# A decoder layer on one Trainium2 core: gate products on another engine, alternating buffers for weight sums, and another rule for when a unit is issued

## The chip, the cores and the metric

The kernel runs on one core of one Trainium2 chip. The metric is the device time of one execution in microseconds (us); three executions of the kernel before took 321.8, 321.82 and 323.23 us, with a median of 321.82 us. The engines of a core are called by the names of the profile: PE (matrix products), PEld (its weight loads, which overlap with PE), DVE (VectorE), ACT (ScalarE), POOL (GpSimd) and SP (here only an issuer of transfers).

## The reference

One decoder layer for 256 tokens of width 1024, all in float32:

```python
h = rms_norm(x)
q, k, v, ga | u, vb, gb | qc, gc | three merge gates = split(h @ w_in)
A = moba_attention(rope(q), rope(k), v) * silu(ga)        # 6 heads of 128
B = gmlp_spatial_gate(u, vb, w_spatial) * silu(gb)        # 6 groups of 128
C = memory_cross_attention(qc, rms_norm(mem) @ w_mem_kv) * silu(gc)   # 4 heads
m = sigmoid(ma) * (A @ w_a) + sigmoid(mb) * (B @ w_b) + sigmoid(mc) * (C @ w_c)
out = rms_norm(x + m @ w_out)
```

The products with `silu(...)` are the gate products of this document (branch B has one more, by the spatially mixed `vb`), and `ma`, `mb`, `mc` are the merge gates.

## The kernel before, in words

**Chunks.** The weights come as pieces of 128 x 2048 values, and each piece is used as two chunks of 128 x 1024, 124 chunks in all. PE's work is a fixed list of these chunks (`plan`): 0 to 3 are the memory's values, 4 to 7 its keys, 8 to 19 the values of A and the `vb` of B by token, 20 to 23 `qc`; then the features q, k, ub, gc, ga and gb two chunks at a time, with pairs of merge-gate chunks ("st") between them; from 88 on the branch projections ("br") with the last merge-gate pairs, and at the end the output projection.

**Splitting.** For precision every product of float32 is done in three passes of a faster type (fp32r): high by high, high by low, low by high. So each chunk is first split: ACT writes its high part (`hi`, L238, a copy into fp32r), then DVE its low part (`lo`, L242, the raw chunk minus `hi`). `hi` and `lo` have four buffers each, raw pieces three, and the program issues a chunk's split three chunks ahead of its products (LEAD). A few small products (transposes L724, scores of the first tokens L773, their values L821, spatial mixing L948) are plain fp32. The products of a chunk are L398 to L400 (by token, and the branch and output projections), L482 (merge gates) and L554 (features).

**Merge gates.** Each of the three gates (g = 0, 1, 2) is computed by a scheme with seven products in place of eight (i = 1, 2, 5, 3, 6, 7, 4 in the order of issue), each a pair of chunks. Products accumulate in two banks; when product 7 of a gate is done, DVE subtracts what the bank then holds from an earlier result (L498, the step called `c22`), and only then may product 4 go on adding in that bank. The sums of weight blocks that the products need are formed by transfers in two buffers, `form0` and `form1`: a block is loaded by SP's queue (L218) or added onto what the buffer holds by GpSimd's queue (L221). Which buffer a product uses is fixed by the product:

```python
    FORMS = {1: (0, 0), 5: (0, 1), 6: (0, 3), 4: (0, 2), 2: (1, 2), 7: (1, 1), 3: (1, 3)}
    BUF = {i: f[0] for i, f in FORMS.items()}
```

So product 4 of a gate and product 1 of the next, which are issued one after the other, both use `form0`, and the second is loaded only when both splits of the first have read it.

**The order of everything else.** All other work is cut into units (an engine, a cost in us, what it comes after, a chunk at which it is due). A planner, `Units`, keeps a clock for each engine while the program is written out: at each chunk it first lets in units of ACT, DVE, POOL and the queues, then the split of the chunk three ahead, then the chunk's products, then units of PE. A unit with its predecessors done is let in when the chunk has reached its due number, or when its engine's clock is at most 2.5 us (POOL 0.5 us) past PE's. Instructions run in the order in which they were written, engine by engine, so that a unit that waits holds back each split behind it.

**The gate products.** Each is over two heads or groups, 128 x 512 values: L959 for C (two of them) and A (three), L604 for B with its silu, L998 for B with the mixing. All eleven run on GpSimd. Their results are split for the branch projections by L964 on ACT (`ah`, `obh`, `och`) and L968 on DVE (`al`, `obl`, `ocl`). The sigmoids of the merge gates are L501 on ACT, and the first of them brings a load of the sigmoid table with it (`ACT_TABLE_LOAD`), because the silus before used another. On the way there also stand L350 and L351 on DVE (`dg`, four small instructions for the memory's norm), L403 (`mvl`, the low part of the memory's values) and L446 on GpSimd (sums of tokens for the merge gates).

The row names are those of the profile: `lo<-form,hi` is the low split of a merge-gate chunk, `lo<-raw,hi` that of any other.

Of the kernel before, what the change touches and what calls it, by code (L numbers as in the profile page):

```python
# [44 lines left out]

ORDER = (1, 2, 5, 3, 6, 7, 4)
# [34 lines left out]
class Units:  # L81
# [30 lines left out]
    def fits(self, u, i, pe, now):  # L112
# [10 lines left out]
        return self.t[e] <= now + (self.ahead if e != POOL else 0.5) and self.ready(after) <= max(now, self.t[e]) + 0.3  # L123
# [17 lines left out]
def tile_hybrid_layer(ctx: ExitStack, tc: tile.TileContext, mw, xT, mem, x, fin_g, ln_g, w, ws, w_sp, b_sp, rope, out):  # L141
# [83 lines left out]
    BUF = {i: f[0] for i, f in FORMS.items()}  # L225

    def form_step(g, i):

        buf, b = FORMS[i]
        return (form_add if i in (5, 6, 4, 7) else form_load, buf, g, b)  # L230
# [163 lines left out]
    U = Units(4.5, 2.5, 0.8)  # L394
# [66 lines left out]
    def mm_st(c):  # L461
# [35 lines left out]
        elif i == 7:  # L497
            later(f"c22{g}", DVE, 0.7, lambda: nc.vector.tensor_tensor(c22, c22, p, OP.subtract), due=c + 2)  # L498
# [44 lines left out]
    def mm_fea(c):  # L543
# [54 lines left out]
        elif name == "gb":  # L598
            g = join_pair(name, h)
            join(g[:, h % 2, :])  # L600
            if h % 2:
                u = V["ub"][:, h - 1:h + 1, :]
                U.chain(f"gbs{h // 2}", (ACT, 0.62, lambda: nc.scalar.activation(g, g, AF.Silu)),
                        (POOL, 1.6, lambda: nc.gpsimd.tensor_tensor(u, u, g, OP.mult)),  # L604
                        after=[f"gb{h - 1}", f"gb{h}", "exps"])
# [331 lines left out]
    U.add("silu", None, 0, lambda: None, after=["gcs", "gas"] + [f"gbs{i}" for i in range(GB // 2)])  # L937
# [20 lines left out]
    def gate_unit(src, g):  # L958
        nc.gpsimd.tensor_tensor(src, src, g, OP.mult)  # L959
# [26 lines left out]
    for i in range(3):  # L986
        hs = slice(2 * i, 2 * i + 2)
        U.add(f"ga_{i}", POOL, 1.6, lambda hs=hs: gate_unit(V["qk"][:, hs, 0, :], V["ga"][:, hs, :]),
              after=[f"av{2 * i}", f"av{2 * i + 1}", "gas"])
        two_split(f"oaT{i}", lambda i=i, hs=hs: (V["qk"][:, hs, 0, :], V["ah"][:, hs, :], V["al"][i]),  # L990
                  [f"ga_{i}", "oaTa"], due=at_br[0, i] - 2)
# [5 lines left out]
    for i in range(3):  # L997
        U.add(f"mg{i}", POOL, 1.6, lambda i=i: nc.gpsimd.tensor_tensor(  # L998
# [3 lines left out]
            after=[f"mix{i}", f"gbs{i}"])  # L1002
# [118 lines left out]
    for c in range(n_br):  # L1121
        if chunks[c][0] == "st" and chunks[c][3] == 0:
            buf = BUF[chunks[c][2]]
            at = free[buf] + 1
            dma.setdefault(at, []).append(form_step(*chunks[c][1:3]))
            ready[c // 2] = at
            free[buf] = c + 2 - LEAD
    pace = lambda c: 5.0 + sum({"fea": 2.78, "st": 1.365}.get(k[0], 2.73) for k in chunks[:c])
    for c, at in ready.items():
        ready[c] = pace(at) + (10.0 if chunks[2 * c][2] in (4, 5, 6, 7) else 6.0)  # L1130
    for c in range(n_br + 4):
# [25 lines left out]
        U.end[f"c{c}"] = U.run(PE, {"fea": 2.78, "st": 1.365}.get(kind, 2.73), U.end.get(f"s{c}", 0.0))  # L1157
# [126 lines left out]
```

## Time and profile before

| what | value |
|---|---|
| median of three executions | 321.82 us (321.8 to 323.23) |
| the profiled execution's own time | 321.63 us |
| its span in the trace | 319.9 us |
| granted TensorE clock over the span | 0.997 |
| PE | 310.6 us busy, 97% of the span, 1626 products |
| DVE, ACT, POOL | 251.9, 220.9 and 54.8 us busy (79%, 69%, 17%) |
| DMA | 74.37 MB, mean 232 GB/s |

All rows come from the one profiled execution. Its own time is 1.7 us longer than its span, and 0.19 us under the median. The span runs from the first to the last instruction that the profiler saw; stamps are us from its start. A row of the timeline shows the start, the duration, the engine, the line, the operation, and then output and inputs with their shapes; `x2` means that two instructions of a kind were drawn together in a row. A product of 512 columns shows as some 0.39 us long, but products overlap in the engine's pipeline, so the pace of PE is read from start to start. A bracket at a row's end gives the idle time just before it and what ended it.

### The profile page before, as it was taken

The page shows a single profiled execution, that of the slowest core. Times are in us where ns is not written, and L with a number is a line of the kernel's source. Part 1 is how long each engine was busy: PE and PEld are TensorE (multiplying, and loading weights), DVE is VectorE, ACT ScalarE, POOL GpSimd, SP SyncE. Part 2 cuts the span into 40 slices and gives each one's busy share as a digit, 9 for nine tenths or more (in the row PEclk, how much of TensorE's full clock was granted, in tenths as well). Part 3 has the DMA queues.
Part 4 walks back from the last instruction along what each step waited for, and adds up shares of the span by engine and source line. Part 5 has one row for each costly group of instructions (what it writes and reads, how often), then busy time and mean ns, then how long its engine had stood idle before and what let it go on. Part 6 is the DMA issues. An engine that isn't in the chain of part 4 may idle for free.

```text
span 319.9 us, 4510 instructions
## 1 busy us (share of the span) xinstructions
PE 310.6 (97%) x1626; PEld 263.9 (82%) x1626; DVE 251.9 (79%) x362; ACT 220.9 (69%) x362; POOL 54.8 (17%) x54
## 2 busy tenths in 40 slices
PE   8999999999999999999999999999999999999992
PEld 4788888889888888888888889887887888888982
DVE  3989989697579678869687898787969978889452
ACT  4869675664988566787696797776798555656533
POOL 1003820001001110000210453754311110000022
PEclk9999999999999999999999999999999999999998
DMA  7999895846379899488489879567869999673003
GB/s 248 405 422 388 332 364 205 348 143 172 80 241 254 154 224 305 125 280 332 154 190 321 206 204 265 118 254 275 222 228 261 273 234 266 277 265 131 0 15 119
DMA packets 14855, 74.37 MB, mean 232 GB/s; under 512 B 1904, under 2 KB 3056, under 8 KB 8176
## 3 DMA queue, kind: packets, MB, share of 16 engines
q1 hardware_dynamic: 12816, 61.16, 52.0%
q0 software_dynamic: 1728, 12.58, 21.0%
q10 hardware_dynamic: 288, 0.33, 0.3%
q8 instruction: 13, 0.21, 0.3%
q14 instruction: 10, 0.08, 0.1%
HBM read 72.23 MB, written 1.05 MB: 229 GB/s over the span
## 4 chain that ended last, share of the span: by engine, by line
PE 82%; DMA 5%; DVE 5%; ACT 3%; issue 3%; POOL 1%; SPq 0%; ACTq 0%; DVEq 0%
PE acc L554 31%; PE acc L482 11%; PE acc L399 8%; PE acc L400 8%; PE acc L398 8%; PE aux L482 5%; DMA xk<-in_x_dram 3%; PE aux L399 2%; PE aux L398 2%; PE aux L400 2%; DVE lo L242 2%; DMA st<-in_mw_dram 2%; PE aux L724 2%; PE aux L948 1%; ACT hi L238 1%
## 5 line engine op out<-in xcount | busy, mean ns | idle before, releaser
L242 DVE TENSOR_TENSOR lo<-raw,hi 128x1024 fp32r<-128x1024 f32 x78 | 99.2, 1283 | 32.1 <-ACT hi L238 30.8
L238 ACT ACTIVATE hi<-raw 128x1024 fp32r<-128x1024 f32 x78 | 82.0, 1058 | 24.4 <-PE acc L400 18.4
L554 PE MATMUL acc<-n,hi 128*128 128x512 f32 x304 | 80.0, 393 | 0.0
L554 PEld LDWEIGHTS acc<-n,hi 128*128 128x128 f32 x304 | 55.5, 189 | 9.6
L242 DVE TENSOR_TENSOR lo<-form,hi 128x1024 fp32r<-128x1024 f32 x42 | 55.5, 1336 | 9.6 <-ACT hi L238 9.3
L238 ACT ACTIVATE hi<-form 128x1024 fp32r<-128x1024 f32 x42 | 43.9, 1053 | 4.2 <-DMA form<-in_ws_dram 1.9
L554 PEld LDWEIGHTS acc<-n,lo 128*128 128x128 f32 x304 | 41.5, 190 | 3.0
L554 PE MATMUL acc<-n,lo 128*128 128x256 f32 x304 | 42.4, 282 | 0.0
L221 POOL DMA_DIRECT2D form<-in_ws_dram x12 | 10.6, 883 | 158.4 <-DVE lo L242 152.6
L482 PE MATMUL acc<-hi,s 128*128 128x512 f32 x64 | 21.9, 397 | 0.0
L399 PE MATMUL acc<-lo,n 128*128 128x512 f32 x48 | 18.8, 392 | 0.2 <-DVE lo L242 0.2
L398 PE MATMUL acc<-hi,n 128*128 128x512 f32 x48 | 18.7, 390 | 0.0
L400 PE MATMUL acc<-hi,n 128*128 128x512 f32 x48 | 18.7, 389 | 0.0
L482 PE MATMUL acc<-hi,n 128*128 128x512 f32 x48 | 16.6, 400 | 0.7 <-DVE sigs L498 0.7
L482 PEld LDWEIGHTS acc<-hi,s 128*128 128x128 f32 x64 | 12.0, 188 | 2.3
L1095 POOL TENSOR_TENSOR xk<-xk,fing 128x512 f32<-128x512 f32 (+1 forms) x4 | 4.0, 1010 | 51.8 <-ACT jk L1091 51.8
L562 ACT ACTIVATE qk<-acc 128x256 f32<-128x256 f32 x12 | 4.7, 388 | 11.6 <-PE acc L554 11.6
L482 PE MATMUL acc<-lo,s 128*128 128x512 f32 x32 | 12.5, 391 | 0.0
L482 PEld LDWEIGHTS acc<-hi,n 128*128 128x128 f32 x48 | 9.0, 188 | 2.7 <-ACT jt L562 1.0
L562 ACT ACTIVATE jt<-acc 128x256 f32<-128x256 f32 x14 | 5.3, 380 | 8.4 <-PE acc L554 8.3
L399 PEld LDWEIGHTS acc<-lo,n 128*128 128x128 f32 x48 | 9.0, 188 | 2.4 <-DVE lo L242 0.6
L400 PEld LDWEIGHTS acc<-hi,n 128*128 128x128 f32 x48 | 9.0, 188 | 1.9
(236 smaller groups left out, 627.7 us busy)
## 6 DMA issues: line engine op xcount, KB each, us to landing
raw<-in_w_dram SPq DMA_DIRECT2D x30, 1024.0 KB, 6.1
form<-in_ws_dram POOLq DMA_DIRECT2D x12, 1024.0 KB, 8.6
raw<-in_w_dram SPq DMA_DIRECT2D x18, 512.0 KB, 7.5
form<-in_ws_dram SPq DMA_DIRECT2D x9, 1024.0 KB, 4.9
st<-in_mw_dram SPq DMA_DIRECT2D x6, 384.0 KB, 7.2
xk<-in_x_dram SPq DMA_DIRECT2D x2, 512.0 KB, 8.8
xt<-in_xT_dram SPq DMA_DIRECT2D x2, 512.0 KB, 10.1
mm<-in_mem_dram SPq DMA_DIRECT2D x2, 512.0 KB, 11.6
```

The costliest lines, as they stand in the source:

```text
L221: nc.gpsimd.dma_start(form_tile(i), block(g, b), accum_op=OP.add)
L238: nc.scalar.activation(hi[c][:, a:b], raw[c // 2][:, o + a:o + b], AF.Copy)
L242: nc.vector.tensor_tensor(lo[c][:, a:b], raw[c // 2][:, o + a:o + b], hi[c][:, a:b].bitcast(F32), OP.subtract)
L398: nc.tensor.matmul(p, s_hi, m_hi, start=first, stop=False)
L399: nc.tensor.matmul(p, s_hi, m_lo, start=False, stop=False)
L400: nc.tensor.matmul(p, s_lo, m_hi, start=False, stop=last)
L482: nc.tensor.matmul(p, x[:, k0 + k, tsl(t)], wt[c][:, a * 512:(a + 1) * 512], start=first and a + j == 0, stop=half == 1 and a + j == 3, sk ...
L554: nc.tensor.matmul(o, wt, m, start=i == 0, stop=i == len(passes) - 1)
L562: nc.scalar.activation(dst, pa, AF.Copy)
L724: nc.tensor.transpose(p[:, hsl(j)], src, ident)
L948: nc.tensor.matmul(pv[:, a, t, :], V["vb"][:, t, hsl(g)], V["wsp"][:, g, :], start=True, stop=True)
L1095: nc.gpsimd.tensor_tensor(z, z, V["fing"][:, a:b], OP.mult)
```

## The change

It does five things.

1. The eleven gate products (L604, L959, L998) are written for VectorE in place of GpSimd, with a planned cost of 0.69 us in place of 1.6 us, and get due chunks. The high and low splits of A's results (L964, L968) get earlier due chunks.
2. The two buffers of weight sums swap roles in every second gate: the buffer is that of the product, exclusive-or the gate's number modulo 2.
3. The planner's limit for letting in a unit is no longer 2.5 us: it is worked out from the time of the next three chunks on PE (`room`), less 2.4 us for ACT or 1.3 us for DVE, less 1.2 us (`AHEAD`), less the unit's cost, but at least 0.3 us. POOL keeps 0.5 us.
4. Product 7's subtraction (L498 before, L502 after) is due one chunk sooner, and the load of the sigmoid table becomes a unit of its own (L941 after). The number of table loads stays the same.
5. In the plan the pair `ub0`, `ub1` comes ahead of a merge-gate pair and of `q5`, `k5` (chunks 42 to 47).

```diff
+SPAN = {"fea": 2.78, "st": 1.365}
+AHEAD = 1.2
...
-    for what in ("q0", "", "q1", "", "q2", "", "q3", "", "q4", "", "q5", "ub0", "", "gc0", "", "gc2", "ub2", "",
+    for what in ("q0", "", "q1", "", "q2", "", "q3", "", "q4", "ub0", "", "q5", "", "gc0", "", "gc2", "ub2", "",
...
-        return self.t[e] <= now + (self.ahead if e != POOL else 0.5) and self.ready(after) <= max(now, self.t[e]) + 0.3
+        lead = 0.5 if e == POOL else max(0.3, self.room - (2.4 if e == ACT else 1.3) - self.ahead - us)
+        return self.t[e] <= now + lead and self.ready(after) <= max(now, self.t[e]) + 0.3
...
-    BUF = {i: f[0] for i, f in FORMS.items()}
+    def buf(g, i):
+        return FORMS[i][0] ^ (g % 2)
...
-    U = Units(4.5, 2.5, 0.8)
+    U = Units(4.5, AHEAD, 0.8)
...
-            later(f"c22{g}", DVE, 0.7, lambda: nc.vector.tensor_tensor(c22, c22, p, OP.subtract), due=c + 2)
+            later(f"c22{g}", DVE, 0.7, lambda: nc.vector.tensor_tensor(c22, c22, p, OP.subtract), due=c + 1)
...
-                        (POOL, 1.6, lambda: nc.gpsimd.tensor_tensor(u, u, g, OP.mult)),
-                        after=[f"gb{h - 1}", f"gb{h}", "exps"])
+                        (DVE, 0.69, lambda: nc.vector.tensor_tensor(u, u, g, OP.mult)),
+                        after=[f"gb{h - 1}", f"gb{h}", "exps"], due=c + 4)
...
-    U.add("silu", None, 0, lambda: None, after=["gcs", "gas"] + [f"gbs{i}" for i in range(GB // 2)])
+    U.add("silu", ACT, 1.4, lambda: nc.scalar.preload_act_table(AF.Sigmoid), after=["gcs", "gas"] + [f"gbs{i}" for i in range(GB // 2)])
...
     def gate_unit(src, g):
-        nc.gpsimd.tensor_tensor(src, src, g, OP.mult)
+        nc.vector.tensor_tensor(src, src, g, OP.mult)
...
-        U.add(f"ga_{i}", POOL, 1.6, lambda hs=hs: gate_unit(V["qk"][:, hs, 0, :], V["ga"][:, hs, :]),
-              after=[f"av{2 * i}", f"av{2 * i + 1}", "gas"])
+        U.add(f"ga_{i}", DVE, 0.69, lambda hs=hs: gate_unit(V["qk"][:, hs, 0, :], V["ga"][:, hs, :]),
+              after=[f"av{2 * i}", f"av{2 * i + 1}", "gas"], due=chunks.index(("st", 2, 1, 0)) - 8)
...
-        U.add(f"mg{i}", POOL, 1.6, lambda i=i: nc.gpsimd.tensor_tensor(
+        U.add(f"mg{i}", DVE, 0.69, lambda i=i: nc.vector.tensor_tensor(
...
-            after=[f"mix{i}", f"gbs{i}"])
+            after=[f"mix{i}", f"gbs{i}"], due=chunks.index(("fea", "gb", 2 * i + 1)) + 5)
...
+        U.room = sum(SPAN.get(k[0], 2.73) for k in chunks[c:c + LEAD])
```

Line numbers of the kernel after are mostly those of before plus 4: the high and low splits L238 and L242 become L242 and L246, L498 becomes L502, L604 becomes L608, L964 and L968 become L968 and L972, and L998 becomes L1002.

What the new rules make of the order is shown at three places; a fourth is told in words: in the token pass (chunks 8 to 19) VectorE has the reciprocal L344 and the four `dg` instructions now ahead of the low split of chunk 12, and the two `mvl` instructions ahead of that of chunk 14, where they stood behind the splits of chunks 14, 19 and 17. The first place is VectorE, before, around chunk 82, the first half of product 4 of gate 1. The two rows `lo<-form_510` are the low splits of chunks 82 and 83, and L498 is the subtraction that must have read the bank before chunk 82's products add to it.

```order
L968 TENSOR_TENSOR al_2200<-qk,ah 128x512
L242 TENSOR_TENSOR lo<-raw,hi 128x1024
L242 TENSOR_TENSOR lo<-form_510,hi 128x1024 x2
L564 TENSOR_TENSOR jt<-jt,acc 128x256
L498 TENSOR_TENSOR sigs_1726<-sigs_1726,acc 128x512
L242 TENSOR_TENSOR lo<-raw,hi 128x1024
L564 TENSOR_TENSOR jt<-jt,acc 128x256
```

VectorE after, at the same place.

```order
L972 TENSOR_TENSOR al_2161<-qk,ah 128x512
L246 TENSOR_TENSOR lo<-raw,hi 128x1024
L972 TENSOR_TENSOR al_2161<-qk,ah 128x512
L972 TENSOR_TENSOR al_2162<-qk,ah 128x512
L246 TENSOR_TENSOR lo<-form_643,hi 128x1024
L502 TENSOR_TENSOR sigs_1758<-sigs_1758,acc 128x512
L246 TENSOR_TENSOR lo<-form_643,hi 128x1024
L568 TENSOR_TENSOR jt<-jt,acc 128x256
L608 TENSOR_TENSOR ub<-ub,jt 128x512
L246 TENSOR_TENSOR lo<-raw,hi 128x1024
```

The subtraction now stands between the two low splits in place of behind both and a sum of features; two low splits of A have come in ahead of it, and a gate product (L608) stands behind it.

The second place is ScalarE, before, around chunk 93, the second half of a branch piece. The last row but one is the high split of chunk 93, the second row that of chunk 92; `obh` reads a gate product, and the three L501 rows behind the table load are sigmoids.

```order
L238 ACTIVATE hi<-form_636 128x1024
L238 ACTIVATE hi<-raw 128x1024
L964 ACTIVATE obh<-ub 128x512
L501 ACT_TABLE_LOAD
L501 ACTIVATE sig_858<-sig_858 128x1024
L501 ACTIVATE sig_859<-sig_859 128x1024
L501 ACTIVATE sigs_1726<-sigs_1726 128x1024
L238 ACTIVATE hi<-raw 128x1024
L238 ACTIVATE hi<-form_510 128x1024 x2
```

ScalarE after, at the same place.

```order
L242 ACTIVATE hi<-form_643 128x1024
L242 ACTIVATE hi<-raw 128x1024
L941 ACT_TABLE_LOAD
L505 ACTIVATE sig_852<-sig_852 128x1024
L242 ACTIVATE hi<-raw 128x1024
L968 ACTIVATE obh<-ub 128x512
L505 ACTIVATE sig_853<-sig_853 128x1024
L242 ACTIVATE hi<-form_523 128x1024 x2
L242 ACTIVATE hi<-raw 128x1024
```

Between the high splits of chunks 92 and 93 there are now the table load and one sigmoid, in place of a cast, the table load and three sigmoids.

The third place is TensorE, before, in the middle of A's attention: three kinds of plain fp32 products (L821, L724, L773) in a row.

```order
L400 MATMUL aux<-pth,v_450 128x256
L821 MATMUL aux<-pt_1714,v_451 128x128
L724 MATMUL aux<-ident,p 128x128 x3
L773 MATMUL aux<-qk 128x128
L398 MATMUL aux<-qh 128x256
```

TensorE after, a little further on in the same work: the first product of a head's scores (L777, plain fp32), the three fp32r ones, and the same for the next head.

```order
L777 MATMUL aux<-qk 128x128
L402 MATMUL aux<-qh 128x256
L403 MATMUL aux<-ql,qh 128x256
L404 MATMUL aux<-qh,ql 128x256
L777 MATMUL aux<-qk 128x128
L402 MATMUL aux<-qh 128x256
```

The products are the same ones in both kernels, but the plain ones stand together less often: counted over the whole of TensorE's order, an fp32r product follows a plain one 19 times before and 22 times after.

More of the change, by code (lines that the diff above doesn't have):

```diff
@@ L89, in __init__ @@
         self.t, self.ahead, self.margin = [start] * 5, ahead, margin
-        self.todo, self.end = [], {}
+        self.todo, self.end, self.room = [], {}, 0.0
     def add(self, name, e, us, fn, after=(), first=False, wait=0.0, due=10 ** 6):
@@ L224, in tile_hybrid_layer @@
     FORMS = {1: (0, 0), 5: (0, 1), 6: (0, 3), 4: (0, 2), 2: (1, 2), 7: (1, 1), 3: (1, 3)}
[L225 removed]
+    def buf(g, i):
+        return FORMS[i][0] ^ (g % 2)
     def form_step(g, i):
[L229 to L230 removed]
+        return (form_add if i in (5, 6, 4, 7) else form_load, buf(g, i), g, FORMS[i][1])
     def split_alloc(c):
@@ L987, in tile_hybrid_layer @@
         hs = slice(2 * i, 2 * i + 2)
-        U.add(f"ga_{i}", POOL, 1.6, lambda hs=hs: gate_unit(V["qk"][:, hs, 0, :], V["ga"][:, hs, :]),
-              after=[f"av{2 * i}", f"av{2 * i + 1}", "gas"])
+        U.add(f"ga_{i}", DVE, 0.69, lambda hs=hs: gate_unit(V["qk"][:, hs, 0, :], V["ga"][:, hs, :]),
+              after=[f"av{2 * i}", f"av{2 * i + 1}", "gas"], due=chunks.index(("st", 2, 1, 0)) - 8)
         two_split(f"oaT{i}", lambda i=i, hs=hs: (V["qk"][:, hs, 0, :], V["ah"][:, hs, :], V["al"][i]),
-                  [f"ga_{i}", "oaTa"], due=at_br[0, i] - 2)
+                  [f"ga_{i}", "oaTa"], due=chunks.index(("st", 2, 1, 0)) - 6 + i)
     U.add("ocTa", None, 0, alloc(("och", [128, HC, S], "och", F32R), ("ocl", [128, HC, S], "ocl", F32R)),
@@ L1010, in tile_hybrid_layer @@
         hs = slice(2 * i, 2 * i + 2)
-        U.add(f"gc_{i}", POOL, 1.6, lambda hs=hs: gate_unit(V["oc"][:, hs, :], V["gc"][:, hs, :]),
-              after=[f"cv{2 * i}", f"cv{2 * i + 1}", "gcs"])
+        U.add(f"gc_{i}", DVE, 0.69, lambda hs=hs: gate_unit(V["oc"][:, hs, :], V["gc"][:, hs, :]),
+              after=[f"cv{2 * i}", f"cv{2 * i + 1}", "gcs"], due=chunks.index(("st", 2, 1, 0)) - 8)
         two_split(f"ocT{i}", lambda hs=hs: (V["oc"][:, hs, :], V["och"][:, hs, :], V["ocl"][:, hs, :]),
@@ L1122, in tile_hybrid_layer @@
         if chunks[c][0] == "st" and chunks[c][3] == 0:
-            buf = BUF[chunks[c][2]]
-            at = free[buf] + 1
+            b = buf(*chunks[c][1:3])
+            at = free[b] + 1
             dma.setdefault(at, []).append(form_step(*chunks[c][1:3]))
             ready[c // 2] = at
-            free[buf] = c + 2 - LEAD
-    pace = lambda c: 5.0 + sum({"fea": 2.78, "st": 1.365}.get(k[0], 2.73) for k in chunks[:c])
+            free[b] = c + 2 - LEAD
+    pace = lambda c: 5.0 + sum(SPAN.get(k[0], 2.73) for k in chunks[:c])
     for c, at in ready.items():
@@ L1143, in tile_hybrid_layer @@
             if chunks[e][0] == "st":
-                raw[e // 2] = form_tile(BUF[chunks[e][2]])
+                raw[e // 2] = form_tile(buf(*chunks[e][1:3]))
                 came = ready[e // 2]
@@ L1156, in tile_hybrid_layer @@
         kind = chunks[c][0]
-        U.end[f"c{c}"] = U.run(PE, {"fea": 2.78, "st": 1.365}.get(kind, 2.73), U.end.get(f"s{c}", 0.0))
+        U.end[f"c{c}"] = U.run(PE, SPAN.get(kind, 2.73), U.end.get(f"s{c}", 0.0))
         if kind == "tok":
```

## The prediction

> **What bounds the kernel now.** I read the page's first lines, then the busy time by stage.
>
> ```profile
> span 319.9 us, 4510 instructions
> PE 310.6 (97%) x1626; PEld 263.9 (82%) x1626; DVE 251.9 (79%) x362; ACT 220.9 (69%) x362; POOL 54.8 (17%) x54
> 30.00:210.00 180.00, 180.00 (x1002) 156.67 (x1001) 143.80 (x224) 131.79 (x237) 32.21 (x28) 1.00 0.76 230
> 210.00:250.00 40.00, 38.83 (x185) 32.18 (x184) 35.33 (x37) 30.36 (x38) 12.57 (x8) 1.00 0.79 245
> 250.00:300.00 50.00, 50.00 (x237) 41.81 (x236) 41.87 (x48) 29.19 (x33) 1.72 (x2) 1.00 0.71 222
> ```
>
> The lower rows give a stretch of the span and its length, then the busy time of PE, PEld, DVE, ACT and POOL, the granted clock, the DMA share and GB/s. PE is busy without a gap from 30 to 210 and from 250 to 300 us, at full clock. Between 210 and 250 it loses 40.00 − 38.83 = 1.17 us. So the change can only win where PE waits, and only lose by making it wait or by giving it more to do. Next the timeline of PE in that stretch, for the rows around its gaps.
>
> ```profile
> 216.61 0.39 PE L554 MATMUL acc<-n,hi 128*128 128x512 f32 x1
> 217.70 0.47 PE L482 MATMUL acc<-hi,n 128*128 128x512 f32 x1 [0.70 <-DVE sigs L498]
> ...
> 239.50 0.39 PE L400 MATMUL acc<-hi,al 128*128 128x512 f32 x1
> 239.73 0.39 PE L398 MATMUL acc<-hi,obh 128*128 128x512 f32 x1
> 240.59 0.50 PE L399 MATMUL acc<-lo,obh 128*128 128x512 f32 x1 [0.47 <-DVE lo L242]
> 240.93 0.39 PE L400 MATMUL acc<-hi,obl 128*128 128x512 f32 x1
> ```
>
> The undisturbed pace of a 512-column product is 239.73 − 239.50 = 0.23 us from start to start. The first stall is 217.70 − 216.61 − 0.23 = 0.86 us, the second 240.59 − 239.73 − 0.23 = 0.63 us, and 240.93 − 240.59 − 0.23 = 0.11 us comes right behind it. Together they are 1.60 us, more than the idle time, since a stall also empties the pipeline. I looked for other long steps in PE's starts: between 30 us and the tail there is nothing over 0.1 us but these.
>
> Last the chain of waits for this stretch (start, duration, work), the steps that lead into the two stalls, and the DVE and POOL timelines ahead of the first.
>
> ```profile
> 216.96 0.61 DVE sigs L498
> ...
> 230.25 1.46 POOL ub L604
> 231.79 1.63 POOL ub L998
> ...
> 234.07 1.28 ACT L501
> ...
> 237.28 1.04 ACT sigs L501
> 238.32 0.96 ACT hi L238
> ```
> ```profile
> 212.07 4.55 DVE L242 TENSOR_TENSOR lo<-form,hi 128x1024 fp32r<-128x1024 f32 x2
> ```
> ```profile
> 211.16 2.15 POOL L604 TENSOR_TENSOR ub<-ub,jt 128x512 f32<-128x512 f32 x1 [5.46 <-ACT jt L603]
> 213.39 2.15 POOL L998 TENSOR_TENSOR ub<-ub,mt 128x512 f32<-128x512 f32 x1
> ```
>
> First stall: the subtraction L498 stands behind two low splits that took 4.55 us while GpSimd did two gate products. Second stall: the low split of chunk 93 is late because its high split is late; that stands on ACT behind a cast that waited for GpSimd (L604, then L998, to 233.42), the table load and three sigmoids, and starts only at 238.32.
>
> **The change part by part.** First the groups on VectorE beside GpSimd's gate products (186.5 to 237 us, four rows: busy us and mean ns behind the bar), and as the last row the low splits without GpSimd (255 to 295 us). Below them the busy time of two stretches.
>
> ```profile
> L242 DVE TENSOR_TENSOR lo<-form,hi 128x1024 fp32r<-128x1024 f32 x12 | 19.2, 1621 | 3.9 <-ACT hi L238 3.9
> L242 DVE TENSOR_TENSOR lo<-raw,hi 128x1024 fp32r<-128x1024 f32 x11 | 14.4, 1312 | 2.3 <-ACT hi L238 2.2
> L968 DVE TENSOR_TENSOR obl<-ub,obh 128x512 fp32r<-128x512 f32 x2 | 2.5, 1231 | 0.0
> L968 DVE TENSOR_TENSOR al<-qk,ah 128x512 fp32r<-128x512 f32 x3 | 2.0, 679 | 0.0
> ...
> L242 DVE TENSOR_TENSOR lo<-form,hi 128x1024 fp32r<-128x1024 f32 x6 | 7.2, 1222 | 0.3
> ```
> ```profile
> 187.00:205.00 18.00, 18.00 (x109) 15.89 (x109) 15.70 (x21) 13.85 (x20) 10.70 (x7) 1.00 0.97 246
> 205.00:241.00 36.00, 34.83 (x174) 29.11 (x173) 29.59 (x30) 27.62 (x37) 12.40 (x8) 1.00 0.70 232
> ```
>
> *The products on VectorE.* Added: 11 of 128x512; the nearest row is `al`, same shape and two inputs, 0.679 us, so 11 × 0.68 = 7.5 us. Taken back: 12 × (1.621 − 1.222) + 11 × (1.312 − 1.222) + 2 × (1.231 − 0.679) = 4.8 + 1.0 + 1.1 = 6.9 us. Net +0.6 us against an idle time of (18.00 − 15.70) + (36.00 − 29.59) = 8.7 us, so nothing on PE's path. What hides it is the lead of three chunks; without relief the 7.5 us nearly fill the 8.7 us (a rival below).
>
> The Trainium skill ("SBUF — State Buffer", section "Who interferes with whom") has a rule on this: a VectorE instruction with two inputs in SBUF and a GpSimd instruction lock each other out of a shared pair of ports, so that the second waits until the first is done. By it each product would give back its whole length, an estimate of 11 × 1.29 = 14 us, taking GpSimd's undisturbed product from the row here:
>
> ```profile
> L1095 POOL TENSOR_TENSOR xk<-xk,fing 128x512 f32<-128x512 f32 x2 | 2.6, 1289 | 50.3 <-ACT jk L1091 50.3
> ```
>
> The trace agrees in kind (1.62 us beside it, 1.22 us without), not in full; by either price VectorE is relieved enough, and the sum stays.
>
> *The first stall.* In the order after, L502 stands between the low splits of chunks 82 and 83. Counted on from 212.07, where chunk 81's split is done, with undisturbed durations: two `al` splits, one low split and the subtraction are 2 × 0.68 + 1.22 + 0.61 = 3.2 us, so about 215.3 us. Product 7's sums themselves come no later than before. PE wants the bank at 216.61 + 0.23 = 216.84 us: 1.5 us to spare. Gain 0.86 us; at worst (another unit in front costs over 1.5 us) nothing.
>
> *The second stall.* The row of the high split of chunk 92:
>
> ```profile
> 231.82 1.06 ACT L238 ACTIVATE hi<-raw 128x1024 fp32r<-128x1024 f32 x1 [0.70 <-ACT hi L238]
> ```
>
> It ends at 232.88. In the order after, the table load (1.28 us) and one sigmoid (1.04 us) follow and then the high split of chunk 93, which so may start at 235.2 in place of 238.32 us, 3.1 us sooner. Its low split was 0.63 us late; so it is now some 2.5 us early, less what VectorE has taken on by then (one or two products, 0.7 to 1.4 us): over 1 us remains. Gain 0.63 + 0.11 = 0.74 us; at worst nothing. Late next would be the chunks right behind 93, whose splits queue behind the same instructions; they come forward with them.
>
> *The buffers that swap.* ACT's one wait for a form transfer lay under PE's chunks 84 and 85 and cost PE nothing (no gap is near it), so its going is worth nothing. Loads now come by turns in the two buffers; SP's queue is not the later one at any PE gap. From 0 to −0.1 us; I take 0.
>
> *PE's own order.* An fp32r product right after a plain one starts late. Rows at one such place:
>
> ```profile
> 171.27 0.38 PE L821 MATMUL aux<-pt,v 128*128 128x128 f32 x2
> 171.40 0.48 PE L482 MATMUL acc<-hi,n 128*128 128x512 f32 x1
> 171.72 0.40 PE L482 MATMUL acc<-lo,n 128*128 128x512 f32 x1
> ```
>
> 171.72 − 171.40 = 0.32 us where 0.23 is the pace: 0.09 us each time. With 22 such places in place of 19, 3 × 0.09 = +0.27 us, which nothing hides. Bounds: 0 (a place beside a wait) to +0.5 us (if a switch also costs on its other side).
>
> *Token pass, chunks 8 to 19.* Ahead of chunk 14's low split now stand four `dg`, a reciprocal and two `mvl`. Rows:
>
> ```profile
> 34.73 5.92 DVE L242 TENSOR_TENSOR lo<-raw,hi 128x1024 fp32r<-128x1024 f32 x3 [0.79 <-ACT hi L238]
> ...
> 41.17 0.15 DVE L344 RECIPROCAL rstm<-rts 128x2 f32<-128x2 f32 x1
> ...
> 47.58 1.40 DVE L403 SCALAR_TENSOR_TENSOR mvl<-aux,rstm,cx 128x512 fp32r<-128x512 f32 x2
> ...
> 53.39 0.28 DVE L350 TENSOR_SCALAR dg<-ident,rstm 128x128 fp32r<-128x128 f32 x1
> 53.71 0.35 DVE L351 SCALAR_TENSOR_TENSOR dg<-ident,rstm,dg 128x128 fp32r<-128x128 f32 x1
> ```
> ```profile
> 45.20 0.39 PE L399 MATMUL acc<-lo,n 128*128 128x512 f32 x1
> 32.88 8.93 POOL L446 TENSOR_TENSOR xt<-xt 128x512 f32<-128x512 f32 x4 [6.23 <-DVE n L406]
> ```
>
> Chunk 14's split is the last of the three and ended at 34.73 + 5.92 = 40.65; PE wanted it at 45.20, so 4.55 us are to spare. Moved ahead of it: 2 × (0.28 + 0.35) + 0.15 + 1.40 = 2.8 us, up to 3.9 us if GpSimd's sums (to 41.8) stretch these as they stretched the splits (5.92 against 3 × 1.22 = 3.66). 0.7 to 1.7 us stay: nothing on the path. Chunks 42 to 47 have full lead in a stage with no gap: 0.
>
> *Sum.* 321.63 − 0.86 − 0.74 + 0.27 = 320.3 us against the profiled execution. The median stands 0.19 us above it, so 320.5 us.
>
> **The rivals.**
>
> *One stall stays.* For it: both spares (1.5 and over 1 us) are no longer than one or two instructions of VectorE, and the order after puts products in just these places. Against: each spare is counted with the added instructions in front. If the first stays, 320.5 + 0.86 = 321.4; if the second, 321.2 us; if one half goes, less. 321.3 us.
>
> *A new wait in the token pass.* For it: the reciprocal now stands ahead of chunk 12, and waits for the memory's norm on ACT; each us of that wait eats the same 4.55 us. If it waits past 1.7 us, PE stands at chunk 12 to 15, some 0.5 to 1 us: 321.0 to 321.5 us, so 321.3.
>
> *VectorE becomes the bound (slower).* Place: 187 to 241 us. If its splits stay as long as they are now, because something other than GpSimd stretched them (the DMA share is 0.97 in the first stretch), 7.5 us come on top. The idle time is in pieces before and behind, and a late chunk has some 2.5 us of lead (as worked out for chunk 93), so 7.5 − 2.5 = 5.0 us would reach PE: 320.5 + 5.0 = 325.5 us. It decides from where new waits pass 2.9 us (323.4). Against it: the pair of splits at 212.07 took 2.3 us each while GpSimd's two products ran, in a stretch with a DMA share of 0.70, and from 255 to 295 us, where the share is 0.71 and GpSimd idle, the mean is 1.222.
>
> *PE has headroom.* The Trainium skill ("Perfetto Trace Analysis", "Identifying the Most-Contended Engine") says that busy products mislead and that the weight loads' share is the better measure. The page here gives PEld 82%, so by it a fifth of the span could still be won by feeding PE better. The rows that bear on it:
>
> ```profile
> L554 PEld LDWEIGHTS acc<-n,hi 128*128 128x128 f32 x304 | 55.5, 189 | 9.6
> ```
>
> A load takes 0.189 us of a pace of 0.23 us, and 0.189 / 0.23 = 82% is what full pace gives, so nothing remains. If the pace still quickened by 1%, 317.3 us.
>
> **How the numbers follow.** A measurement of this kernel can tell about 0.5% from no change, 1.6 us: faster is under 320.2, slower over 323.4 us.
>
> Forecast (both stalls go, three switches more): 0.66, 320.5 us, of its own 320.0 to 321.0 (the switches from 0 to 0.5 us, and 0.2 us of an execution to another). One stall stays: 0.15, 321.3. Token pass: 0.07, 321.3. VectorE the bound: 0.10, 325.5. Headroom: 0.02, 317.3. The bound at 320.2 lies 0.3 us below the forecast, inside its own range; I give 0.26 of its 0.66 to faster, where the switches cost nothing or another short wait goes as well. So faster 0.26 + 0.02 = 0.28; slower 0.10; the same 0.62. The range 320.0 to 321.7 us holds the forecast (some 0.60 of it) and the two cases at 321.3 us (0.22).
>
> **What would show it.** In the profile after: no step over 0.15 us in PE's starts between 30 us and the tail, but 22 of 0.08 to 0.09 us; low splits of 1.22 to 1.3 us from 187 to 237 us; L502 done ahead of 216.8 us; the high split of chunk 93 before 236 us; no product of 128x512 on POOL from 187 to 237 us. Wrong is the forecast if PE's row names DVE or ACT between 187 and 250 us or at chunks 12 to 15, or if low splits stay at 1.6 us.

## The result and the profile after

The kernel after takes 320.38 us (median of 6 executions, 320.16 to 320.94), the kernel before 321.87 us (median of 6, 321.78 to 323.23): a ratio of 0.9948, with a 95% interval of 0.993 to 0.9966. That is 1.49 us less. The prediction said 320.5 us, in a range of 320.0 to 321.7 us. The outcome it held likeliest was a time between 320.2 and 323.4 us, and the measured one lies 0.2 us inside that bound. That the point was met so closely is luck in part, since its errors nearly cancel: a new wait of 0.69 us that it did not expect, against an old stall of 0.66 us that its trace had not shown and 0.27 us for switches of PE that cost next to nothing.

The page's first lines after, and the busy time of the three stages (PE, PEld, DVE, ACT, POOL, clock, DMA share, GB/s):

```profile
span 318.7 us, 4501 instructions
PE 310.9 (98%) x1626; PEld 264.4 (83%) x1626; DVE 252.5 (79%) x373; ACT 221.0 (69%) x362; POOL 33.5 (11%) x43
30.00:210.00 180.00, 179.58 (x999) 156.13 (x998) 145.57 (x231) 130.74 (x236) 21.78 (x23) 1.00 0.74 228
210.00:250.00 40.00, 40.00 (x193) 33.71 (x192) 35.22 (x43) 31.44 (x39) 2.58 (x3) 1.00 0.84 274
250.00:300.00 50.00, 50.00 (x237) 41.84 (x236) 40.55 (x47) 30.20 (x33) 0.86 (x1) 1.00 0.65 204
```

The idle 1.17 us between 210 and 250 us are gone. In their place 0.42 us are idle in the first of the three stretches, where the kernel before had none. The timelines at chunk 82 (VectorE, then PE):

```profile
213.47 1.22 DVE L246 TENSOR_TENSOR lo<-form,hi 128x1024 fp32r<-128x1024 f32 x1
214.61 0.68 DVE L502 TENSOR_TENSOR sigs<-sigs,acc 128x512 f32<-128x512 f32 x1
```
```profile
217.12 0.40 PE L558 MATMUL acc<-n,hi 128*128 128x512 f32 x1
217.35 0.40 PE L486 MATMUL acc<-hi,n 128*128 128x512 f32 x1
```

The subtraction is done at 214.61 + 0.68 = 215.29 us, and PE goes on at its pace of 0.23 us. The second place, ScalarE from the high split of chunk 92 to that of chunk 93, and PE there:

```profile
231.36 1.06 ACT L242 ACTIVATE hi<-raw 128x1024 fp32r<-128x1024 f32 x1 [0.18 <-ACT hi L242]
232.44 1.28 ACT L941 ACT_TABLE_LOAD   x1
233.74 1.06 ACT L505 ACTIVATE sig<-sig 128x1024 f32<-128x1024 f32 x1
234.70 1.04 ACT L242 ACTIVATE hi<-raw 128x1024 fp32r<-128x1024 f32 x1
```
```profile
239.28 0.39 PE L402 MATMUL acc<-hi,obh 128*128 128x512 f32 x1
239.50 0.39 PE L403 MATMUL acc<-lo,obh 128*128 128x512 f32 x1
```

Chunk 93's high split starts at 234.70 us in place of 238.32, and there is no wait. The new one is at chunk 12. PE, then VectorE, then GpSimd:

```profile
39.51 0.39 PE L402 MATMUL acc<-hi,n 128*128 128x512 f32 x1
40.32 0.50 PE L403 MATMUL acc<-lo,n 128*128 128x512 f32 x1 [0.42 <-DVE lo L246]
40.65 0.39 PE L404 MATMUL acc<-hi,n 128*128 128x512 f32 x1
```
```profile
33.79 0.17 DVE L348 RECIPROCAL rstm<-rts 128x2 f32<-128x2 f32 x1
33.99 0.95 DVE L354 TENSOR_SCALAR dg<-ident,rstm 128x128 fp32r<-128x128 f32 x1
34.98 1.40 DVE L355 SCALAR_TENSOR_TENSOR dg<-ident,rstm,dg 128x128 fp32r<-128x128 f32 x1
36.30 1.39 DVE L354 TENSOR_SCALAR dg<-ident,rstm 128x128 fp32r<-128x128 f32 x1
37.72 1.40 DVE L355 SCALAR_TENSOR_TENSOR dg<-ident,rstm,dg 128x128 fp32r<-128x128 f32 x1
39.05 2.44 DVE L246 TENSOR_TENSOR lo<-raw,hi 128x1024 fp32r<-128x1024 f32 x2
```
```profile
32.64 6.34 POOL L450 TENSOR_TENSOR xt<-xt 128x512 f32<-128x512 f32 x4 [6.23 <-DVE n L410]
```

The four `dg` instructions took 0.28 and 0.35 us each before, 1.26 us together; here they stand beside GpSimd's sums and take 37.72 + 1.40 − 33.99 = 5.1 us, so that chunk 12's low split starts at 39.05 and PE waits (40.32 − 39.51 − 0.23) + (40.65 − 40.32 − 0.23) = 0.58 + 0.10, some 0.69 us.

### The profile page after: what moved, and what is told of

Its sections match the earlier page's. It is cut to its first block, busy times and chain, and to the rows that moved or that the text cites. A ratio compares the mean times of both kernels' runs of the same rounds, so it can differ in the third digit from the quotient of the medians.

```text
span 318.7 us, 4501 instructions
## 1 busy us (share of the span) xinstructions
PE 310.9 (98%) x1626; PEld 264.4 (83%) x1626; DVE 252.5 (79%) x373; ACT 221.0 (69%) x362; POOL 33.5 (11%) x43
## 3 DMA queue, kind: packets, MB, share of 16 engines
q0 software_dynamic: 1728, 12.58, 20.7%
## 4 chain that ended last, share of the span: by engine, by line
PE 85%; DMA 8%; ACT 2%; DVE 2%; issue 1%; ACTq 0%; SPq 0%; DVEq 0%
PE acc L558 33%; PE acc L486 12%; PE acc L403 8%; PE acc L404 8%; PE acc L402 8%; DMA raw<-in_w_dram 6%; PE aux L486 6%; PE aux L404 2%; PE aux L403 2%; PE aux L402 2%; PE aux L728 2%; DMA st<-in_mw_dram 1%; ACT hi L242 1%; PE aux L952 1%; DVE lo L246 1%; DVE dg L354 1%
## 5 line engine op out<-in xcount | busy, mean ns | idle before, releaser
L246 DVE TENSOR_TENSOR lo<-raw,hi 128x1024 fp32r<-128x1024 f32 x78 | 94.5, 1220 | 25.8 <-ACT hi L242 25.1
L242 ACT ACTIVATE hi<-raw 128x1024 fp32r<-128x1024 f32 x78 | 82.2, 1056 | 24.8 <-PE acc L404 18.4
L558 PE MATMUL acc<-n,hi 128*128 128x512 f32 x304 | 80.9, 395 | 0.0
L246 DVE TENSOR_TENSOR lo<-form,hi 128x1024 fp32r<-128x1024 f32 x42 | 52.1, 1250 | 9.6 <-ACT hi L242 9.1
L242 ACT ACTIVATE hi<-form 128x1024 fp32r<-128x1024 f32 x42 | 43.9, 1055 | 2.6 <-PE aux L486 1.5
L486 PE MATMUL aux<-hi,s 128*128 128x512 f32 x32 | 10.5, 389 | 0.0
```

Source lines behind the costliest of these rows:

```text
L242: nc.scalar.activation(hi[c][:, a:b], raw[c // 2][:, o + a:o + b], AF.Copy)
L246: nc.vector.tensor_tensor(lo[c][:, a:b], raw[c // 2][:, o + a:o + b], hi[c][:, a:b].bitcast(F32), OP.subtract)
L486: nc.tensor.matmul(p, x[:, k0 + k, tsl(t)], wt[c][:, a * 512:(a + 1) * 512], start=first and a + j == 0, stop=half == 1 and a + j == 3, sk ...
L558: nc.tensor.matmul(o, wt, m, start=i == 0, stop=i == len(passes) - 1)
```

## The experiments

All ratios are to the kernel before, timed beside it on the same chip; its median was 321.87 us in the first round and 321.99 to 322.04 us in the later ones, so that times of different rounds compare to some 0.2 us. A step is the time from the start of one product of PE to that of the next. "Start" below is what PE's steps up to 30 us take in all beyond the usual (median) step of a product of the same shape in the first trace of the kernel before. The tail, from the start of the last product to the end, is 6.39 to 6.41 us in every trace but one.

**Memory norm held back (late_norm).**

```diff
-    U.chain("mrms", *rms_all("m", rstm), after=["mrow"])
+    U.chain("mrms", *rms_all("m", rstm), after=["mrow", "c15"])
```

> The kernel after, with the memory norm's unit (the reciprocal is its own unit and stays; the four dg instructions) let in only after chunk 15, so that it stands behind the low splits as in the kernel before. Theory A (the four dg instructions, stretched from 1.26 to 5.1 us while GpSimd does its four sums of tokens, make the low split of chunk 12 late): PE's step of 0.81 us at chunk 12 becomes 0.23 us and the 0.11 us behind it goes, 0.69 us in all, so 320.38 - 0.69 = 319.7 us. Rival B (chunk 12 is late because its raw weights or its high split are late, since PE now comes there sooner than before): the step stays and the time stays at 320.4 us.

Measured: 319.71 us (319.44 to 319.95), ratio 0.9927 [0.9912, 0.9942], 0.67 us under the kernel after. PE at chunk 12:

```profile
39.11 0.39 PE L402 MATMUL acc<-hi,n 128*128 128x512 f32 x1
39.34 0.39 PE L403 MATMUL acc<-lo,n 128*128 128x512 f32 x1
```

Theory A holds, and rival B falls. A smaller wait, 0.27 us, shows at 126.85 us, where chunk 45's low split stands behind a wait for a transfer of the rotation of q and k; in the kernel after that split came in time by 0.2 us. So PE's steps past 30 us account for 0.69 − 0.27 = 0.42 us of the 0.67, and a shorter start (1.71 us against 1.86) for 0.15.

**GpSimd's sums on VectorE (sums_on_dve).**

```diff
-            nc.gpsimd.tensor_tensor(o, a, b, op)
+            nc.vector.tensor_tensor(o, a, b, op)
```

> The kernel after, with the four sums of tokens (the only GpSimd work from 32 to 39 us) issued on VectorE at the place in the program where they were issued on GpSimd, behind the low split of chunk 12. The dg instructions stay ahead of chunk 12. Theory A: dg is back at 0.28 and 0.35 us each, the low split of chunk 12 ends near 36.5 us in place of 40.3, no step over 0.15 us at chunks 12 to 15, 319.7 us; the four sums take 0.68 us each. Rival B (raw weights or high split late): the step at chunk 12 stays, 320.4 us. Rival C (VectorE has no room in the token pass): a wait at chunk 13 or 14 in its place, 320.4 us or more.

VectorE at the same place:

```profile
34.13 0.29 DVE L354 TENSOR_SCALAR dg<-ident,rstm 128x128 fp32r<-128x128 f32 x1
34.46 0.35 DVE L355 SCALAR_TENSOR_TENSOR dg<-ident,rstm,dg 128x128 fp32r<-128x128 f32 x1
...
35.31 1.22 DVE L246 TENSOR_TENSOR lo<-raw,hi 128x1024 fp32r<-128x1024 f32 x1
```

The mechanism is shown: with nothing on GpSimd the `dg` are back at 0.29 and 0.35 us, the low split of chunk 12 ends at 36.53 us, and no wait is left. The time does not show it as clearly: 320.21 us (319.68 to 320.76), ratio 0.9943 [0.9927, 0.9959]. The profiled execution, 320.64 us, had a start of 2.20 us and a tail of 6.88 us, each 0.5 us more than with late_norm; why the tail is longer is open.

**Products on VectorE, nothing else (engine_only).** The kernel before with `nc.vector` for `nc.gpsimd` in L604, L959 and L998.

> The kernel before, with the eleven gate products issued on VectorE at the places in the program where they were issued on GpSimd, and nothing else changed: planner's costs, buffers, rule and order are those of before. Theory A (GpSimd beside VectorE stretched the splits that made the first stall, and the wait for GpSimd only adds to a queue on ACT that is too long anyway): the first stall goes (0.86 us), of the second stall's 0.74 us more than half stays, since three sigmoids and the table load still stand ahead of chunk 93's high split; no wait at chunk 12; 19 steps of 0.09 us: 321.87 - 0.86 - 0.3 = 320.7 us. Rival C (VectorE is crowded by 7.5 us of products and only the new order makes room): new waits between 187 and 241 us, 322 us or more.

Measured: 328.35 us (327.75 to 329.37), ratio 1.0195 [1.0173, 1.0217]. Rival C holds, far above the 322 us from which it counted. PE between chunks 92 and 93, and what ScalarE and VectorE did ahead of it:

```profile
240.35 0.39 PE L400 MATMUL acc<-hi,al 128*128 128x512 f32 x1
243.59 0.58 PE L398 MATMUL acc<-hi,obh 128*128 128x512 f32 x1 [2.85 <-ACT hi L238]
244.85 0.80 PE L399 MATMUL acc<-lo,obh 128*128 128x512 f32 x1 [0.68 <-DVE lo L242]
```
```profile
232.78 1.05 ACT L238 ACTIVATE hi<-raw 128x1024 fp32r<-128x1024 f32 x1
237.71 0.63 ACT L964 ACTIVATE obh<-ub 128x512 fp32r<-128x512 f32 x1 [3.88 <-DVE ub L998]
```
```profile
235.85 1.22 DVE L242 TENSOR_TENSOR lo<-raw,hi 128x1024 fp32r<-128x1024 f32 x1
236.99 0.68 DVE L998 TENSOR_TENSOR ub<-ub,mt 128x512 f32<-128x512 f32 x1
```

VectorE is not too busy (28.29 of 36 us from 205 to 241). The cast `obh` on ScalarE waits 3.88 us for a product that is now in VectorE's queue, behind low splits and other work; behind the cast stand the table load, three sigmoids and chunk 93's high split; and VectorE then waits 5.89 us for that. Read from these rows, the two queues hold each other up. The first stall does not go either: the product behind the one at 216.81 us comes 1.5 us late, for the subtraction, where it was 0.87 us late before. And behind the longest wait PE's granted clock is halved:

```profile
245.00:248.00 3.00, 3.00 (x7) 2.33 (x8) 3.00 (x4) 2.33 (x3) 0.58 (x1) 0.50 0.67 218
```

**Products back on GpSimd, and the subtraction back (pool_products, c22_late, c22_late_pool).** Three kernels, each the kernel after with: the products on GpSimd at a cost of 1.6 us; the subtraction due `c + 2`; both.

```diff
-            later(f"c22{g}", ..., due=c + 1)
+            later(f"c22{g}", ..., due=c + 2)
...
-        nc.vector.tensor_tensor(src, src, g, OP.mult)
+        nc.gpsimd.tensor_tensor(src, src, g, OP.mult)
```

> The kernel after, with the eleven gate products back on GpSimd at the planner's old cost of 1.6 us, and the rest of the change kept (due chunks, swapped buffers, new rule, earlier subtraction and table load). Theory A (the move to VectorE is what ends the first stall, by ending the stretch): low splits of 1.6 us again between 187 and 237 us and at least one of the two stalls back, 320.38 + 0.6 to 1.6 = 321.0 to 322.0 us. Rival D (the order alone ends both stalls: the subtraction one split earlier, the high split behind one sigmoid): stretched splits, but no stall past 200 us, 320.4 us.

> The kernel after, with the subtraction behind product 7 due one chunk later, as before: it stands behind both low splits of product 4 and a sum of features; products stay on VectorE. Theory E (the order ends the first stall, the engine only helps): unstretched, the subtraction moves back by 1.22 + 0.41 us and PE waits 0.1 to 0.4 us at chunk 82, 320.5 to 320.8 us. Theory A as in the prediction (the end of the stretch alone ends it): no wait at chunk 82, 320.4 us.

> Both undone: the kernel after, with the subtraction due one chunk later and the eleven products on GpSimd. With the products on GpSimd alone PE waited 0.30 us at chunk 82. Theory E: the subtraction is now behind a stretched split more, the wait is 0.9 us or more, the whole first stall is back, 321.2 us or more; it takes both, stretch and order, to make it. Rival: the wait stays at 0.3 us, so that neither made the first stall.

| | subtraction early | subtraction late |
|---|---|---|
| products on VectorE | 320.38 us, no wait at chunk 82 | 320.47 us, no wait |
| products on GpSimd | 320.61 us, wait 0.30 us | 322.28 us, wait 1.76 us |

The ratios are 0.9948 [0.993, 0.9966] and 0.9957 [0.9941, 0.9974] above, 0.9954 [0.9937, 0.997] and 1.0017 [1.0007, 1.0028] below. VectorE and PE with both undone:

```profile
214.26 3.45 DVE L246 TENSOR_TENSOR lo<-form,hi 128x1024 fp32r<-128x1024 f32 x2
217.63 0.41 DVE L568 TENSOR_TENSOR jt<-jt,acc 128x256 f32<-128x256 f32 x1
217.97 0.68 DVE L502 TENSOR_TENSOR sigs<-sigs,acc 128x512 f32<-128x512 f32 x1
```
```profile
216.80 0.39 PE L558 MATMUL acc<-n,hi 128*128 128x512 f32 x1
218.79 0.47 PE L486 MATMUL acc<-hi,n 128*128 128x512 f32 x1 [1.60 <-DVE sigs L502]
```

In the order of the kernel after it takes both, GpSimd's products and the late subtraction, to make the first stall, and either part of the change ends all or most of it: the move 1.76 us, the earlier subtraction 1.46 us, both 1.76 us. In the order of before the move alone does not end it (1.5 us in engine_only), so this holds only with the rest of the change in place. The forecast of c22_late (0.1 to 0.4 us of wait) was too high: the subtraction ended at 216.78 us, 0.6 us ahead of PE. In none of the three is there a step over 0.15 us at chunk 93. So the new order ends the second stall with the products on GpSimd as well, and the move without the order does not (engine_only). In pool_products that high split stands behind the table load, a cast and one sigmoid, and starts at 235.56 us.

The low splits of merge-gate chunks beside GpSimd's products are longer in pool_products than in the kernel before, 1.96 us in the mean against 1.62:

```profile
L246 DVE TENSOR_TENSOR lo<-form,hi 128x1024 fp32r<-128x1024 f32 x12 | 23.3, 1959 | 0.6 <-ACT hi L242 0.6
```

And yet PE loses only the 0.30 us at chunk 82 to them, and the kernel takes 320.61 us. So nearly the whole gain comes from the order. The move to VectorE adds those 0.30 us at most, and the times, 0.23 us apart, do not separate it from nothing. Which part of the order ends the second stall (the new rule or the table load as a unit of its own) was not tried apart, and neither were the swapped buffers and the moved pair of chunks.

**The old rule up to chunk 23 (old_rule_early).**

```diff
+        if i < 24 and e != POOL:
+            lead = 2.5
```

> The kernel after, with the old rule (2.5 us ahead, for ACT and VectorE) up to chunk 23, so that the token pass is in the order of before, the reciprocal behind chunk 14's low split included; the new rule from chunk 24 on. Theory A (only the dg instructions beside GpSimd's sums made the wait at chunk 12): no step over 0.15 us at chunks 12 to 15, 319.7 us as with the norm held back. Theory S (the change also gains some 0.5 us at the very start, by the order of the first stage, since the stalls that went and came account for only half of the gain): with the old order up to chunk 23 that gain goes, 320.2 us or more, and PE reaches chunk 8 later than 27.8 us.

Measured: 319.77 us (319.4 to 320.21), ratio 0.9937 [0.9923, 0.9951]; no step over 0.1 us past 30 us. Theory A again, from another side: it was the new rule that let the memory's norm in too early. The start was 1.74 us, no worse than the 1.86 us of the kernel after, so that theory S has no support.

**More traces of both (before_again, before_third, after_again).** The waits explained 0.87 + 0.74 − 0.69 = 0.92 us of a gain of 1.5, and 0.65 us with the 0.27 us for three switches that the expectations take off.

> The kernel before once more, for a second trace. The steps of PE past 30 us account for 0.64 us of the gain of some 1.5 us. Theory V (the two stalls differ from run to run, and the first trace had small ones): the sum of the two stalls is over 2 us here, with a start (the steps over the normal pace up to 30 us) that is shorter than the first trace's 2.08 us. Theory S (the start is slower in the kernel before): the start is near 2.08 us again, and the stalls near 1.6 us.

> The kernel before, for a third trace: as for the second. By theory V the sum of the stalls in the three traces spreads by more than 0.5 us; by theory S it is within 0.2 us of 1.6 us, and the start within 0.3 us of 2.08 us.

> The kernel after once more, for a second trace: the wait at chunk 12 is 0.5 to 0.7 us again, no other step over 0.15 us past 30 us. By theory V the start is anywhere from 1.2 to 2.1 us, as in the other traces; by theory S it is near the first trace's 1.62 us.

The two stalls are the same in all three traces of before (0.87 and 0.74 us to 0.01). So theory V, as put, falls. But both new traces of before have a third stall, of 0.66 us at chunk 72, which the first had not. PE, VectorE and GpSimd in the third trace:

```profile
191.06 1.75 PE L554 MATMUL acc<-n,hi 128*128 128x512 f32 x7
193.21 0.39 PE L554 MATMUL acc<-n,lo 128*128 128x256 f32 x1 [0.40 <-DVE lo L242]
```
```profile
188.73 4.42 DVE L242 TENSOR_TENSOR lo<-raw,hi 128x1024 fp32r<-128x1024 f32 x1
```
```profile
189.23 2.83 POOL L959 TENSOR_TENSOR mid<-mid,gc 128x512 f32<-128x512 f32 x2
```

The same split and the same two products in the first trace:

```profile
189.02 1.23 DVE L242 TENSOR_TENSOR lo<-raw,hi 128x1024 fp32r<-128x1024 f32 x1
```
```profile
189.52 4.11 POOL L959 TENSOR_TENSOR mid<-mid,gc 128x512 f32<-128x512 f32 x2
```

The offset between the two starts is 0.5 us in both; one time GpSimd is slow (4.11 us for two) and the split quick, the other time GpSimd is quick and the split waits for both. Times of the three: 321.63, 322.65 and 322.03 us; start 2.10, 2.44 and 1.82 us. The second trace of the kernel after: 320.33 us, wait at chunk 12 of 0.67 us, start 1.70 us, against 0.69 and 1.86 us in the first. Two more kernels give PE the very same products in the order of before, engine_only and gc_on_dve (below), and their starts are 1.48 and 1.28 us. So the start spreads by 1.2 us within one order, more than the 0.5 us that theory S puts down to the change.

The Trainium skill ("SBUF — State Buffer", section "Who interferes with whom") says that a VectorE instruction with two inputs in SBUF shares a read port with GpSimd, that the one that comes second waits for the whole of the first, and that the order of issue decides which one that is. The two traces agree with it in that either side can be the one that waits; that the split which started 0.5 us sooner waits in one of them is not what the rule as stated gives. For the `dg` the length is near: the first took 0.95 us, each of the other three 1.39 to 1.40 us, beside sums of 6.34 / 4 = 1.59 us. But L354 has only one 128x128 tensor among its inputs, so that the rule as told here speaks for L355 alone.

**Two products only (gc_on_dve).** The kernel before, with branch C's two products (L959 on `mid`) on VectorE.

> The kernel before, with only the two gate products of branch C (L959 on mid and gc) issued on VectorE in place of GpSimd, at the places where they were issued. In two of the three traces of the kernel before PE waited 0.66 us at chunk 72, whose low split took 4.4 us beside these two. Theory A: the splits of chunks 72 and 73 take 1.2 us, no step over 0.15 us between 185 and 200 us, the two stalls of 0.86 and 0.74 us stay, and the median, in which the third stall is mostly there, falls by 0.4 to 0.7 us to 321.3 to 321.6 us. Rival C (as in the run with all eleven on VectorE, a cast on ACT now waits for a product behind a split): a wait of 0.5 us or more between 190 and 205 us, 322 us or more.

Measured: 323.31 us (322.79 to 324.62), ratio 1.0045 [1.0031, 1.0059]; slower, so theory A's time is missed. Its first part holds: the splits of chunks 72 and 73 took 1.23 and 1.22 us, and PE did not wait from 185 to 200 us. So the third stall came from these two products on GpSimd. Rival C has the time right and the place wrong, since PE did not wait from 190 to 205 us. But VectorE waited twice 1.65 us for high splits that stood behind casts of the moved products, and from there on VectorE's work stayed late against PE's. PE at chunk 82, and the clock behind it:

```profile
215.77 0.39 PE L554 MATMUL acc<-n,hi 128*128 128x512 f32 x1
218.53 0.47 PE L482 MATMUL acc<-hi,n 128*128 128x512 f32 x1 [2.37 <-DVE sigs L498]
```
```profile
218.50:222.50 4.00, 3.97 (x11) 3.18 (x12) 3.09 (x4) 0.80 (x2) 1.90 (x1) 0.60 0.91 354
```

The first stall grew from 0.87 to 218.53 − 215.77 − 0.23 = 2.53 us, and eight slow products after it cost 8 × 0.20 = 1.6 us (the clock is 0.50 from 219.5 to 222.5 us). This was one of the longer executions, 324.11 us at a mean clock of 0.988; seven of the ten took 322.79 to 323.39 us at 0.994 to 0.999, so the median probably holds the longer stall and not the slow products: 2.53 − 0.87 − 0.66 = 1.0 us of the 1.27 us that it lies above the kernel before. That a lag is carried on from 197 to 218 us is read from these rows, not tested.

**A version that beats both (best).** old_rule_early, with the planned landing time ahead of the rotation raised from 5.0 to 7.5 us, and in even heads the plain product of the scores behind the three fp32r ones.

> The kernel after, with the old rule up to chunk 23; with the planned time of the transfer ahead of the rotation of q and k raised from 5 to 7.5 us, so that chunk 45's low split stands ahead of it and not behind (it left 0.16 us of a wait there); and with the plain fp32 product of an even head's scores issued behind its three fp32r ones, so that two heads' plain products stand together and an fp32r product follows a plain one 20 times, not 22. Expected: no step over 0.15 us past 30 us but the one at chunk 9's start, 20 steps of 0.09 us, 319.7 - 0.2 - 0.2 = 319.3 us. If a step of 0.09 us belongs to something other than the switch from plain fp32 to fp32r, there are still 22 of them and 319.5 us.

Measured: 319.35 us (319.24 to 319.82), ratio 0.9929 [0.9913, 0.9944]. All six times lie under the six of the kernel after, though the intervals of the two ratios overlap a little. PE has no gap in any of the three stretches:

```profile
30.00:210.00 180.00, 180.00 (x1002) 156.70 (x1002) 145.68 (x233) 131.60 (x238) 24.72 (x23) 1.00 0.77 231
210.00:250.00 40.00, 40.00 (x193) 33.71 (x192) 35.32 (x41) 31.10 (x38) 2.59 (x3) 1.00 0.85 269
250.00:300.00 50.00, 50.00 (x242) 42.04 (x241) 40.50 (x46) 29.43 (x33) 0.86 (x1) 1.00 0.63 198
```

The order has 20 switches and PE's starts past 30 us have 20 steps of 0.08 to 0.10 us, where the kernel after has 22 of both; so those steps belong to the switches. But a switch costs next to nothing, which the prediction and this expectation overlooked. Rows of the kernel before at one of them:

```profile
165.81 0.49 PE L724 MATMUL aux<-ident,p 128*128 128x128 f32 x3
166.14 0.39 PE L773 MATMUL aux<-qk 128*128 128x128 f32 x2
166.28 0.36 PE L398 MATMUL aux<-qh 128*128 128x256 f32 x1
166.49 0.28 PE L399 MATMUL aux<-ql,qh 128*128 128x256 f32 x1
```

Among themselves plain instructions of 128 columns take 0.11 us each (166.14 − 165.81 = 0.33 us for three), but the last one ahead of the fp32r product takes 0.14 − 0.11 = 0.03 us only. So the fp32r product starts 0.08 us early, and the 0.21 us to the next start, in place of the usual 0.12, give that back. Over all 19 switches of the kernel before and the 22 of the kernel after, the two steps together come to 0.007 us more than usual for each switch. So the version's gain on old_rule_early does not come from two switches fewer: of the 0.36 us between the two profiled executions, 0.24 us are the start (1.50 us against 1.74) and 0.09 us a last long step at chunk 45.

## Why the prediction was right, and where it was not

- *The bound and the two stalls.* Right. L502 was predicted to end at 215.3 us and ended at 215.29; chunk 93's high split was predicted at 235.2 us and started at 234.70. The whole of it, 0.87 (0.86 in the prediction's rounded stamps) and 0.74 us, is gone.
- *Why they go.* Half right. The relief of VectorE is there (low splits of 1.220 us in place of 1.312 for raw pieces, 1.321 in place of 1.621 for sums, a little above the 1.22 to 1.3 us foretold), but it is not the main cause: the order alone, with the products on GpSimd and the splits stretched to 1.96 us, leaves 0.30 us of the first stall and none of the others (no such step in the traces of pool_products and c22_late_pool), while the move alone makes the stalls longer. The 6.9 us that the prediction counted on VectorE are also only one side of what the two engines lost: in the same trace GpSimd's products took 5.8 + 5.7 + 5.1 + 4.1 = 20.7 us, 6.5 us over 11 × 1.29 = 14.2 us. Together that is 13.4 us, close to the prediction's estimate of 14 us.
- *PE's order.* Right in the count, wrong in the price. There are 22 steps of 0.08 to 0.10 us, as counted from the order. But the term of +0.27 us, "which nothing hides", leaves out the step ahead of each, which is 0.08 us shorter than usual; three switches cost 3 × 0.007 = 0.02 us. The prediction's own rows show it: 171.72 − 171.27 = 0.45 us for two plain instructions and an fp32r product, where 2 × 0.11 + 0.23 is 0.45 us too.
- *The token pass.* Wrong, in the step that was summed as "0.7 to 1.7 us stay". It took chunk 14 as the one in danger, though the four `dg` stand ahead of chunk 12, whose split PE wants some 5.5 us sooner (at 39.51 + 0.23 = 39.74 us here; chunk 14's was wanted at 45.20); and it took the stretch of the long splits (5.92 against 3.66, 1.6 times) for the small instructions, which were stretched from 1.26 to 5.1 us, 4 times. The rival "a new wait in the token pass" came true, with 0.69 us in its 0.5 to 1 us, but by another cause than it named (the reciprocal waited less than 0.1 us), and together with the forecast, not in its place, a case to which the prediction gave no chance. By the prediction's own sign, PE's row naming DVE at chunks 12 to 15, its forecast was wrong there.
- *The sum.* It went by one trace, which had missed a stall of 0.66 us that the other two show. With it, and without the price of the switches, the working is 0.87 + 0.74 + 0.66 − 0.69 − 0.02 = 1.56 us, against 1.49 us measured. Without it, and with the wait at chunk 12 and the 0.27 us, it would have been 0.65 us and 321.2 us. The remainder, 0.1 us, lies within what the start differs by from trace to trace (1.2 us in the order of before); with two or three traces of each kernel it can't be said whether the change has a part in it. That the swapped buffers are worth nothing was not tested.
- *VectorE as the bound.* It did not come about here, and rightly had a small chance for this change as a whole. The place and the sign were right for the move alone: 328.35 us, more than its price of 325.5. The mechanism was not: VectorE had idle time left, and the queues waited for each other.

## What to carry to other kernels

A step moved to a faster engine also moves into that engine's queue: ask who waits for its result, and what that waiter holds back. Here the move alone cost 2%, the order alone gained nearly all there was (320.61 us, against 320.38 us with the move), and the move on top of it added 0.3 us at most. Price small instructions of VectorE beside a GpSimd instruction by that instruction's length (here 1.4 us each beside 1.6), not by the stretch that long ones show, and check the spare of the first chunk behind them. Before a long step of PE is given a price, add up the steps around it: a late start can follow an early one. One trace of a kernel with two engines in contention is one outcome: take a second before a gain of under 1% is summed from its waits.

## What the runs showed of the hardware

In the profiled executions PE's granted clock fell to 0.50 after a wait of PE of 2.37 us (gc_on_dve) and of 2.85 us (engine_only), and stayed at its usual 1.00 after one of 1.60 us (c22_late_pool). It fell with a delay: in gc_on_dve the first three products after the wait still came at 0.24 to 0.31 us, the next eight at 0.43 us, 3.4 us in all. So there a wait of about 2.5 us cost 4.1 us. It need not happen each time: the mean granted clock was 0.987 to 0.991 in all five executions of engine_only, but in gc_on_dve 0.988 and 0.989 in two of ten and 0.993 to 0.999 in the others, where eight products at half clock would take off an estimated 0.5 × 3.4 / 322 = 0.005.

VectorE and GpSimd held each other up by 6.9 + 6.5 = 13.4 us around eleven products of 128x512 on GpSimd, against an undisturbed 14.2 us of these products. At the same offset of 0.5 us between two starts it was GpSimd that was slow in one execution and VectorE in another.

A switch from plain fp32 to fp32r products on PE shows as a step of 0.32 us in place of 0.23, and costs 0.007 us, since the step ahead of it is 0.03 us in place of 0.11.
